# Two softmax attentions, one head at a time or a pair of heads at a time

## The chip, the cores and the metric

The kernel runs on one core of a Trainium2 chip. TensorE (PE in the profile, with its weight loads as PEld) multiplies into PSUM; VectorE (DVE), ScalarE (ACT) and GpSimd (POOL) do the element-wise work; SyncE (SP) issues the transfers. The metric is the device time of the whole program in microseconds (us), the median of several runs.

## The reference, cut to what matters

One program computes two transformer blocks on 512 tokens of width 1024. The first has a neighbourhood attention (8 heads of 64) and a gated convolution; the second an RWKV time mix and, in its second layer, a sliding-window attention with sinks (16 query heads of 64 over 4 key heads). Both attentions are plain softmax attentions:

```python
# neighbourhood attention, first block
s = jnp.einsum('brjqhd,brjkhd->bhrjqk', qb, kb).astype(jnp.float32) * (dh ** -0.5)
s = jnp.where(jnp.asarray(mask), s + bias[None], NEG_INF)
p = jax.nn.softmax(s, axis=-1).astype(v.dtype)
o = jnp.einsum('bhrjqk,brjkhd->brjqhd', p, vb)
...
# sliding window of 128 with a sink per head, second block
s = jnp.einsum('bnqkgd,bnskd->bnkgqs', q, kb).astype(jnp.float32) * (ATT_HEAD ** -0.5)
s = jnp.where(valid[None, :, None, None], s, MASK_VALUE)
p = jax.nn.softmax(jnp.concatenate([s, sink], axis=-1), axis=-1)[..., :-1]
o = jnp.einsum('bnkgqs,bnskd->bnqkgd', p.astype(vb.dtype), vb)
```

## The kernel before

Every projection is a chain of matmuls over 128-wide blocks of the contraction. A weight block is split into a high and a low part (tiles `wh`, `wl`, made by ACT and DVE or POOL from the loaded `wr`), and each block product is three matmuls (`mm3`), written to a PSUM tile named `m`. Other products and transposes go to PSUM tiles named `t`. There are four banks of each kind, taken in turn by `PS()`.

The attentions are written as generators, one for each unit of work, and run between the projection matmuls. A small planner (`_Emit`) keeps a model of each engine's time; a unit is resumed when the tiles that it waits for should be ready. `attention(units, depth)` keeps `depth` units going. All that a unit issues is recorded at line 290 (the branch for urgent work), while other work is at line 288; matmuls are at line 377 and transposes at 391. A scheduler then lays out each engine's own list in order; engines meet by semaphores.

A unit is one head `e` (0 or 1) of a pair of heads and one block `j` of 128 queries. The two heads of a pair share tiles of 128 partitions, head 0 in partitions 0 to 63 and head 1 in 64 to 127, so that their products use different parts of the 128 x 128 array. A unit has these steps:

- scores on PE. In the neighbourhood attention (`na_unit`) that is one fp32 matmul with 64 rows (`t<-a,a`, 64x256), in rows 64e of the array. In the window attention (`sw_unit`) it is two matmuls of 128 rows over a stacked high and low part (`t<-kd,a`)
- add the mask or bias, with the row's minimum of the negated scores, on DVE (CUSTOM_DVE_ANT_0 in the profile, ISA in the order; it frees the scores' bank); exp with its sum on ACT; reciprocal and scaling on DVE
- transposes on PE (`t<-cst,h`), and their copy from PSUM on ACT
- values on PE: for each of two key blocks `kc` one fp32 matmul with 64 columns (`t<-h,a` or `t<-h,vsh`, 64 columns by 128), in columns 64e. The first query block of the window attention has one key block.

There are 32 units of the first kind, run while the convolution's projections are made, and 64 of the second. Half of these (`att0`) run beside the last four blocks of the query projection and the first products of the output projection, the other half (`att1`) beside the output projection. The values of a pair of heads collect in one bank (`po`), from which `split` makes the high and low parts.

Of the kernel before, what the change touches and what calls it, by code (L numbers as in the profile page):

```python
# [295 lines left out]
def tile_net(ctx: ExitStack, tc: tile.TileContext, a: dict, out: bass.AP, dbg=None, stop=None):  # L296
# [359 lines left out]
    def na_unit(hp, j, e):  # L656
        hd = 2 * hp + e
        pr = slice(64 * e, 64 * e + 64)

        def unit():  # L660
            if hd not in bias_t:
                bias_t[hd] = bias_p.tile([P, 768], F32, tag="bias", name=nm("bias"))
                dma(out=bias_t[hd], in_=a["bias1"][:, hd * 768 : (hd + 1) * 768])
            qs, ks = qT[hp][pr, j * 128 : (j + 1) * 128], kT[hp][pr, G0[j] * 64 : G0[j] * 64 + 256]
            yield (qs, ks)
            ps = PS()
            mm(ps[:, 0:256], qs, ks)
            s_, st_ = H(), S()

            vt.tensor_tensor_reduce(out=s_, in0=ps[:, 0:256], in1=bias_t[hd][:, VAR[j] * 256 : VAR[j] * 256 + 256],  # L670
                                    scale=-1.0, scalar=-NEG, op0=ADD, op1=ALU.min, accum_out=st_[:, 1:2])
            act.activation(out=s_, in_=s_, func=AF.Exp, scale=-1.0, bias=st_[:, 1:2], accum_out=st_[:, 2:3])
            vt.reciprocal(out=st_[:, 3:4], in_=st_[:, 2:3])
            vt.tensor_scalar(out=s_, in0=s_, scalar1=st_[:, 3:4], scalar2=None, op0=MUL)
            yield (s_,)
            pt = PS()
            for kc in range(2):
                transpose(pt[:, kc * 128 : (kc + 1) * 128], s_[:, kc * 128 : (kc + 1) * 128])
            pT = H()
            copy(pT, pt[:, 0:256])  # L680
            yield (pT,)
            if hp not in po_t:
                po_t[hp] = [PS(), 0]
            po = po_t[hp][0]
            for kc in range(2):
                mm(po[pr, j * 128 : (j + 1) * 128], vg[G0[j] + 2 * kc][:, hd * 64 : hd * 64 + 64],
                   pT[:, kc * 128 : (kc + 1) * 128], kc == 0, kc == 1)
            po_t[hp][1] += 1
            if po_t[hp][1] == 8:
                ya[hp] = split(po)  # L690
# [4 lines left out]
    with tc.tile_pool(name="bpool", bufs=3) as bias_p:  # L695
        att = em.spawn(attention([na_unit(hp, j, e) for hp in range(4) for j in range(4) for e in range(2)], 5))
# [1246 lines left out]
    def sw_unit(n, j, e):  # L1943
        g, hd = n // 2, 2 * n + e
        pr = slice(64 * e, 64 * e + 64)
        k0, nk, m0 = (0, 128, 128) if j == 0 else ((j - 1) * 128, 256, 0)

        def unit():
            while not q_ready[n]:
                yield 0.25  # L1950
            qs, ks = qts[n][e][:, j * 128 : (j + 1) * 128], [t_[:, k0 : k0 + nk] for t_ in kd[g]]
            yield (qs, *ks)
            ps = PS()
            for i in range(2):
                mm(ps[:, 0:nk], qs, ks[i], i == 0, i == 1)

            s_, st_ = HX(), S()
            gp.tensor_copy(s_[:, nk : nk + 1], nsink[:, hd : hd + 1])
            vt.tensor_tensor_reduce(out=s_[:, 0:nk], in0=ps[:, 0:nk], in1=swam[:, m0 : m0 + nk], scale=-1.0,
                                    scalar=nsink[:, hd : hd + 1], op0=ADD, op1=ALU.min, accum_out=st_[:, 1:2])  # L1960
            act.activation(out=s_[:, 0 : nk + 1], in_=s_[:, 0 : nk + 1], func=AF.Exp, scale=-1.0, bias=st_[:, 1:2],
                           accum_out=st_[:, 2:3])
            vt.reciprocal(out=st_[:, 4:5], in_=st_[:, 2:3])
            vt.tensor_scalar(out=s_[:, 0:nk], in0=s_[:, 0:nk], scalar1=st_[:, 4:5], scalar2=None, op0=MUL)
# [183 lines left out]
```

## Time and profile before

| | |
|---|---|
| median of 3 runs | 3024.93 us (3023.22 to 3025.7) |
| profiled execution | 3018.23 us |
| its span in the trace | 3016.5 us |
| PE busy | 2855.6 us, 95% |
| DVE, ACT, POOL busy | 54%, 42%, 23% |
| neighbourhood attention, first score to last value | 84.9 to 144.6 us |
| window attention, first score to last value | 2491.5 to 2606.5 us |

A page of the profile shows each engine's busy time as a share of the span. A matmul's duration includes its way through the array, so that neighbours overlap; what a matmul costs is read as the distance from its start to the next one's start. One fp32 product stands as two records in the trace: 64 fp32 score products or value products of a stretch would be 128 records.

### The profile page before, as it was taken

How to read it: one execution, taken by the hardware profiler on the slowest of the kernel's cores; microseconds unless marked ns; L12 is line 12 of the kernel's file. 1: busy time of each engine (PE TensorE's matmuls, PEld its weight loads, DVE VectorE, ACT ScalarE, POOL GpSimd, SP SyncE). 2: the span in 40 equal slices, each digit the busy share in tenths (PEclk: the TensorE clock that was granted, in tenths of full speed). 3: DMA queues.
4: the chain of work that ended last, by engine and by line, in shares of the span. 5: the costliest groups of instructions: out<-in, count | busy, mean ns of one | idle time of the engine just before them, and what ended most of it. 6: DMA issues, size and time to landing. Idle time of an engine off the chain costs nothing. (4 is left out here: it accounts for less than half of the span.)

```text
span 3016.5 us, 45856 instructions
## 1 busy us (share of the span) xinstructions
PE 2855.6 (95%) x17744; PEld 2458.6 (82%) x17744; DVE 1628.5 (54%) x2920; ACT 1255.9 (42%) x2205; POOL 690.3 (23%) x809
## 2 busy tenths in 40 slices
PE   9999999999999988788889999998999989899998
PEld 7688888889788876557669999998888887788887
DVE  6544543335334496685866765366234566752336
ACT  4533333323433345454455644344233347643333
POOL 0011211111211143464254210011111134321111
PEclk9999999999999999899779999999999999999999
DMA  5233323332334355655465566343334432323334
GB/s 179 79 98 98 119 91 98 98 98 73 103 98 125 109 177 188 186 172 165 136 177 159 187 178 179 112 152 107 98 98 120 128 102 79 99 81 101 106 109 156
DMA packets 179409, 378.32 MB, mean 125 GB/s; under 512 B 57204, under 2 KB 81908, under 8 KB 179192
## 3 DMA queue, kind: packets, MB, share of 16 engines
q1 hardware_dynamic: 179192, 375.40, 41.6%
q8 instruction: 140, 2.29, 0.3%
q14 instruction: 77, 0.63, 0.1%
HBM read 342.04 MB, written 29.36 MB: 123 GB/s over the span
## 5 line engine op out<-in xcount | busy, mean ns | idle before, releaser
L377 PE MATMUL m<-a,wh 128*128 128x256 f32 (+1 forms) x8512 | 2070.5, 335 | 6.7 <-DVE a L288 4.7
L377 PEld LDWEIGHTS m<-a,wh 128*128 128x128 f32 x8512 | 1462.7, 192 | 171.3 <-issue 10.2
L377 PE MATMUL m<-a,wl 128*128 128x256 f32 (+1 forms) x4256 | 1417.5, 333 | 2.5 <-DVE wl L288 2.3
L288 ACT ACTIVATE wh<-wr 128x1024 fp32r<-128x1024 f32 (+2 forms) x585 | 606.5, 1038 | 1214.0 <-PE m L377 842.0
L288 DVE TENSOR_TENSOR wl<-wr,wh 128x1024 fp32r<-128x1024 f32 (+2 forms) x547 | 673.9, 1233 | 467.7 <-ACT wh L288 464.1
L377 PEld LDWEIGHTS m<-a,wl 128*128 128x128 f32 x4256 | 816.0, 192 | 79.3 <-DVE wl L288 3.9
L288 POOL TENSOR_TENSOR a<-a,a 128x256 f32<-128x256 f32 (+5 forms) x319 | 362.4, 1143 | 1562.0 <-ACT a L288 1335.1
L288 DVE TENSOR_TENSOR a<-m,a 128x512 f32<-128x512 f32 (+1 forms) x324 | 208.7, 645 | 638.8 <-PE m L377 620.9
L288 ACT ACTIVATE a<-a 128x512 f32<-128x512 f32 (+6 forms) x531 | 253.4, 494 | 120.0 <-DVE a L288 100.7
L377 PE MATMUL m<-wh,a 128*128 128x512 f32 x800 | 266.8, 408 | 21.8 <-POOL a L288 9.2
L377 PEld LDWEIGHTS m<-wh,a 128*128 128x128 f32 x800 | 154.6, 194 | 61.9 <-POOL a L288 11.7
L288 DVE TENSOR_TENSOR a<-a,a 128x256 f32<-128x256 f32 (+3 forms) x305 | 159.6, 550 | 24.0 <-ACT a L288 17.2
L377 PE MATMUL m<-wl,a 128*128 128x512 f32 x400 | 161.1, 403 | 0.2 <-DVE wl L288 0.2
L288 DVE SCALAR_TENSOR_TENSOR a<-a,vec,a 128x256 f32<-128x256 f32 (+4 forms) x246 | 145.3, 631 | 8.7 <-ACT a L288 8.4
L288 POOL TENSOR_TENSOR a<-h,a 128x256 fp32r<-128x256 f32 x80 | 70.3, 882 | 292.4 <-ACT a L288 276.3
L288 POOL TENSOR_TENSOR wl<-wr,wh 128x1024 fp32r<-128x1024 f32 x38 | 92.6, 2438 | 134.4 <-ACT wh L288 116.7
L377 PE MATMUL t<-a,a 64*128 64x128 f32 (+3 forms) x400 | 83.7, 380 | 28.0 <-DVE a L288 15.8
L288 ACT ACTIVATE a<-t 128x512 f32<-128x512 f32 (+3 forms) x122 | 58.4, 490 | 86.3 <-PE t L377 68.9
L377 PEld LDWEIGHTS t<-a,a 64*128 64x128 f32 (+2 forms) x400 | 53.2, 222 | 49.2 <-ACT a L288 19.0
L377 PEld LDWEIGHTS m<-wl,a 128*128 128x128 f32 x400 | 77.7, 194 | 16.4 <-issue 0.7
L288 ACT ACTIVATE a<-a,vec 128x256 fp32r<-128x256 f32 (+2 forms) x108 | 60.3, 565 | 41.4 <-DVE a L288 39.2
L377 PE MATMUL t<-cst,a 32*32 32x32 f32 (+2 forms) x432 | 34.7, 237 | 41.4 <-POOL a L288 25.3
(109 smaller groups left out, 1616.2 us busy)
## 6 DMA issues: line engine op xcount, KB each, us to landing
wr<-in_ffn_w_in_dram SPq DMA_DIRECT2D x204, 512.0 KB, 3.7
wr<-in_ffn_w_out_dram SPq DMA_DIRECT2D x80, 448.0 KB, 3.4
wr<-in_ffn_w_out_dram SPq DMA_DIRECT2D x48, 512.0 KB, 3.6
wr<-in_w_out_t_dram SPq DMA_DIRECT2D x34, 512.0 KB, 3.7
wr<-in_w_mlp_in_dram SPq DMA_DIRECT2D x32, 512.0 KB, 3.7
wr<-in_w_mlp_out_dram SPq DMA_DIRECT2D x32, 512.0 KB, 3.7
wr<-in_w_gate_dram SPq DMA_DIRECT2D x16, 512.0 KB, 3.6
wr<-in_w_k_dram SPq DMA_DIRECT2D x16, 512.0 KB, 4.4
```

The lines of the kernel that those rows point to most:

```text
L288: return fn(*args, **kw)
L377: nc.tensor.matmul(out_, lhsT=lhsT, rhs=rhs, start=start, stop=stop)
```

## The change

A unit is now a pair of heads. It has the scores of both heads, their softmax, four transposes into one bank (two in the first query block of the window attention), one copy of up to 512 columns in place of two of up to 256, and the value products in the order key block, then head, so that neighbours alternate between the two halves of the array. The copy goes to a tile of the large pool (`A()`) instead of the pool `h`. In the neighbourhood attention the two heads' scores take a bank each; in the window attention they take the two halves of one bank. `depth` goes from 5 heads to 3 pairs, and the pool of the biases from 3 to 4 tiles.

```diff
@@ -653,47 +653,56 @@
     ya = [None] * 4
     bias_t, po_t = {}, {}
 
-    def na_unit(hp, j, e):
-        hd = 2 * hp + e
-        pr = slice(64 * e, 64 * e + 64)
+    def na_unit(hp, j):
+
+        HE = [(e, slice(64 * e, 64 * e + 64)) for e in range(2)]
 
         def unit():
-            if hd not in bias_t:
-                bias_t[hd] = bias_p.tile([P, 768], F32, tag="bias", name=nm("bias"))
-                dma(out=bias_t[hd], in_=a["bias1"][:, hd * 768 : (hd + 1) * 768])
-            qs, ks = qT[hp][pr, j * 128 : (j + 1) * 128], kT[hp][pr, G0[j] * 64 : G0[j] * 64 + 256]
+            for hd in (2 * hp, 2 * hp + 1):
+                if hd not in bias_t:
+                    bias_t[hd] = bias_p.tile([P, 768], F32, tag="bias", name=nm("bias"))
+                    dma(out=bias_t[hd], in_=a["bias1"][:, hd * 768 : (hd + 1) * 768])
+            qs, ks = qT[hp][:, j * 128 : (j + 1) * 128], kT[hp][:, G0[j] * 64 : G0[j] * 64 + 256]
             yield (qs, ks)
-            ps = PS()
-            mm(ps[:, 0:256], qs, ks)
-            s_, st_ = H(), S()
-
-            vt.tensor_tensor_reduce(out=s_, in0=ps[:, 0:256], in1=bias_t[hd][:, VAR[j] * 256 : VAR[j] * 256 + 256],
-                                    scale=-1.0, scalar=-NEG, op0=ADD, op1=ALU.min, accum_out=st_[:, 1:2])
-            act.activation(out=s_, in_=s_, func=AF.Exp, scale=-1.0, bias=st_[:, 1:2], accum_out=st_[:, 2:3])
-            vt.reciprocal(out=st_[:, 3:4], in_=st_[:, 2:3])
-            vt.tensor_scalar(out=s_, in0=s_, scalar1=st_[:, 3:4], scalar2=None, op0=MUL)
-            yield (s_,)
+            pss = [PS(), PS()]
+            for e, pr in HE:
+                mm(pss[e][:, 0:256], qs[pr, :], ks[pr, :])
+            s2, st_ = [H(), H()], S()
+            for e, ps in enumerate(pss):
+
+                vt.tensor_tensor_reduce(out=s2[e], in0=ps[:, 0:256], in1=bias_t[2 * hp + e][:, VAR[j] * 256 : VAR[j] * 256 + 256],
+                                        scale=-1.0, scalar=-NEG, op0=ADD, op1=ALU.min, accum_out=st_[:, e : e + 1])
+                act.activation(out=s2[e], in_=s2[e], func=AF.Exp, scale=-1.0, bias=st_[:, e : e + 1],
+                               accum_out=st_[:, 2 + e : 3 + e])
+            for e in range(2):
+                vt.reciprocal(out=st_[:, 4 + e : 5 + e], in_=st_[:, 2 + e : 3 + e])
+                vt.tensor_scalar(out=s2[e], in0=s2[e], scalar1=st_[:, 4 + e : 5 + e], scalar2=None, op0=MUL)
+            yield tuple(s2)
             pt = PS()
-            for kc in range(2):
-                transpose(pt[:, kc * 128 : (kc + 1) * 128], s_[:, kc * 128 : (kc + 1) * 128])
-            pT = H()
-            copy(pT, pt[:, 0:256])
+            for e in range(2):
+                for kc in range(2):
+                    transpose(pt[:, (2 * e + kc) * 128 : (2 * e + kc + 1) * 128], s2[e][:, kc * 128 : (kc + 1) * 128])
+            pT = A()
+            copy(pT, pt)
             yield (pT,)
             if hp not in po_t:
                 po_t[hp] = [PS(), 0]
             po = po_t[hp][0]
             for kc in range(2):
-                mm(po[pr, j * 128 : (j + 1) * 128], vg[G0[j] + 2 * kc][:, hd * 64 : hd * 64 + 64],
-                   pT[:, kc * 128 : (kc + 1) * 128], kc == 0, kc == 1)
+                for e, pr in HE:
+                    hd = 2 * hp + e
+                    mm(po[pr, j * 128 : (j + 1) * 128], vg[G0[j] + 2 * kc][:, hd * 64 : hd * 64 + 64],
+                       pT[:, (2 * e + kc) * 128 : (2 * e + kc + 1) * 128], kc == 0, kc == 1)
+            free(pT)
             po_t[hp][1] += 1
-            if po_t[hp][1] == 8:
+            if po_t[hp][1] == 4:
                 ya[hp] = split(po)
 
         return unit
 
     yb, mg = [], []
-    with tc.tile_pool(name="bpool", bufs=3) as bias_p:
-        att = em.spawn(attention([na_unit(hp, j, e) for hp in range(4) for j in range(4) for e in range(2)], 5))
+    with tc.tile_pool(name="bpool", bufs=4) as bias_p:
+        att = em.spawn(attention([na_unit(hp, j) for hp in range(4) for j in range(4)], 3))
 
         r2 = A()
         tt(vt, r2, rb, rb, MUL)
@@ -1940,44 +1949,52 @@
 
     so_t = {}
 
-    def sw_unit(n, j, e):
-        g, hd = n // 2, 2 * n + e
-        pr = slice(64 * e, 64 * e + 64)
+    def sw_unit(n, j):
+
+        g = n // 2
         k0, nk, m0 = (0, 128, 128) if j == 0 else ((j - 1) * 128, 256, 0)
 
         def unit():
             while not q_ready[n]:
                 yield 0.25
-            qs, ks = qts[n][e][:, j * 128 : (j + 1) * 128], [t_[:, k0 : k0 + nk] for t_ in kd[g]]
-            yield (qs, *ks)
+            qs, ks = [qts[n][e][:, j * 128 : (j + 1) * 128] for e in range(2)], [t_[:, k0 : k0 + nk] for t_ in kd[g]]
+            yield (*qs, *ks)
             ps = PS()
-            for i in range(2):
-                mm(ps[:, 0:nk], qs, ks[i], i == 0, i == 1)
-
-            s_, st_ = HX(), S()
-            gp.tensor_copy(s_[:, nk : nk + 1], nsink[:, hd : hd + 1])
-            vt.tensor_tensor_reduce(out=s_[:, 0:nk], in0=ps[:, 0:nk], in1=swam[:, m0 : m0 + nk], scale=-1.0,
-                                    scalar=nsink[:, hd : hd + 1], op0=ADD, op1=ALU.min, accum_out=st_[:, 1:2])
-            act.activation(out=s_[:, 0 : nk + 1], in_=s_[:, 0 : nk + 1], func=AF.Exp, scale=-1.0, bias=st_[:, 1:2],
-                           accum_out=st_[:, 2:3])
-            vt.reciprocal(out=st_[:, 4:5], in_=st_[:, 2:3])
-            vt.tensor_scalar(out=s_[:, 0:nk], in0=s_[:, 0:nk], scalar1=st_[:, 4:5], scalar2=None, op0=MUL)
-            yield (s_,)
-            pt = PS()
-            for kc in range(nk // 128):
-                transpose(pt[:, kc * 128 : (kc + 1) * 128], s_[:, kc * 128 : (kc + 1) * 128])
-            pT = H()
-            copy(pT[:, 0:nk], pt[:, 0:nk])
+            s2, st_ = [HX(), HX()], S()
+            for e in range(2):
+                for i in range(2):
+                    mm(ps[:, e * 256 : e * 256 + nk], qs[e], ks[i], i == 0, i == 1)
+            for e in range(2):
+
+                sink, mn, sm = nsink[:, 2 * n + e : 2 * n + e + 1], st_[:, e : e + 1], st_[:, 2 + e : 3 + e]
+                gp.tensor_copy(s2[e][:, nk : nk + 1], sink)
+                vt.tensor_tensor_reduce(out=s2[e][:, 0:nk], in0=ps[:, e * 256 : e * 256 + nk], in1=swam[:, m0 : m0 + nk], scale=-1.0,
+                                        scalar=sink, op0=ADD, op1=ALU.min, accum_out=mn)
+                act.activation(out=s2[e][:, 0 : nk + 1], in_=s2[e][:, 0 : nk + 1], func=AF.Exp, scale=-1.0, bias=mn, accum_out=sm)
+            for e in range(2):
+                vt.reciprocal(out=st_[:, 4 + e : 5 + e], in_=st_[:, 2 + e : 3 + e])
+                vt.tensor_scalar(out=s2[e][:, 0:nk], in0=s2[e][:, 0:nk], scalar1=st_[:, 4 + e : 5 + e], scalar2=None, op0=MUL)
+            yield tuple(s2)
+            pt, nc_ = PS(), nk // 128
+            for e in range(2):
+                for kc in range(nc_):
+                    i = e * nc_ + kc
+                    transpose(pt[:, i * 128 : (i + 1) * 128], s2[e][:, kc * 128 : (kc + 1) * 128])
+            pT = A()
+            copy(pT[:, 0 : 2 * nk], pt[:, 0 : 2 * nk])
             yield (pT,)
             hf, jj = j // 2, j % 2
             if (n, hf) not in so_t:
                 so_t[n, hf] = [PS(), 0]
             po = so_t[n, hf][0]
-            for kc in range(nk // 128):
-                mm(po[pr, jj * 128 : (jj + 1) * 128], vsh[k0 // 128 + kc][:, g * 64 : g * 64 + 64],
-                   pT[:, kc * 128 : (kc + 1) * 128], kc == 0, kc == nk // 128 - 1)
+            for kc in range(nc_):
+                for e in range(2):
+                    i = e * nc_ + kc
+                    mm(po[HP[e], jj * 128 : (jj + 1) * 128], vsh[k0 // 128 + kc][:, g * 64 : g * 64 + 64],
+                       pT[:, i * 128 : (i + 1) * 128], kc == 0, kc == nc_ - 1)
+            free(pT)
             so_t[n, hf][1] += 1
-            if so_t[n, hf][1] == 4:
+            if so_t[n, hf][1] == 2:
                 split_into(zs[n], po[:, 0:256], HALF[hf])
 
         return unit
@@ -1985,13 +2002,13 @@
     pss = gemm_head(a["w_q"], range(4), en_a.xs, en_a.full)
     ws = [q_out(n, pss[n]) for n in range(4)]
     em.until(lambda: all(w_["done"] for w_ in ws))
-    att0 = em.spawn(attention([sw_unit(n, j, e) for n in range(DC) for j in range(2) for e in range(2)], 5))
+    att0 = em.spawn(attention([sw_unit(n, j) for n in range(DC) for j in range(2)], 3))
     for n in range(4, DC):
         ps = PS()
         gemm(ps, a["w_q"], n, (0, 8), en_a.xs, eng=gp)
         q_out(n, ps)
     em.until(lambda: att0["done"])
-    att1 = em.spawn(attention([sw_unit(n, j, e) for n in range(DC) for j in range(2, 4) for e in range(2)], 5))
+    att1 = em.spawn(attention([sw_unit(n, j) for n in range(DC) for j in range(2, 4)], 3))
     o = [A() for _ in range(DC)]
     so = Stat()
     en = Entry("norm_g", 48 + 32)```

No other instruction is added or taken away: the numbers of matmuls and of DVE, POOL and SP instructions are as before, and ACT has 48 fewer. Outside the two attentions every engine's list stands in the order of before. Three places in the lists follow. The numbers behind tile names only tell tiles apart.

PE in the neighbourhood attention of before, some 3 us after the first transposes: `t_834` is the values' bank of the first pair of heads, `h` tiles are the transposed weights of one head and block, `t_839`, `t_849` and `t_861` are scores of one head.

```order
L391 MATMUL t_829<-cst,h_788 128x128 x2
L377 MATMUL t_834<-h_806,a_720 64x128
L377 MATMUL t_834<-h_806,a_722 64x128
L377 MATMUL t_834<-h_814,a_720 64x128
L377 MATMUL t_834<-h_814,a_722 64x128
L377 MATMUL t_839<-a_634,a_453 128x256
L377 MATMUL t_834<-h_822,a_728 64x128
L377 MATMUL t_834<-h_822,a_731 64x128
L377 MATMUL t_849<-a_634,a_453 128x256
L377 MATMUL t_834<-h_827,a_728 64x128
L377 MATMUL t_834<-h_827,a_731 64x128
```

The same place now, with `a_816`, `a_829` and `a_844` the transposed weights of a pair.

```order
L377 MATMUL t_834<-a_816,a_720 64x128 x2
L377 MATMUL t_834<-a_816,a_722 64x128 x2
L391 MATMUL t_839<-cst,h_788 128x128 x2
L391 MATMUL t_839<-cst,h_789 128x128 x2
L377 MATMUL t_846<-a_634,a_453 128x256
L377 MATMUL t_847<-a_634,a_453 128x256
L377 MATMUL t_834<-a_829,a_728 64x128 x2
L377 MATMUL t_834<-a_829,a_731 64x128 x2
L377 MATMUL t_869<-a_641,a_460 128x256
L377 MATMUL t_870<-a_641,a_460 128x256
L377 MATMUL t_834<-a_844,a_731 64x128 x2
```

Before, the first two units' values stood together and then single heads' scores and values took turns; now scores and values always stand as pairs, and pairs take turns. Counted over the whole stage, PE had 19 bursts of scores and 26 of values, in 21 runs between matmuls of the full array; it now has 15 and 14, in 13 runs.

DVE at the same place now: `t_846` and `t_847` are the scores of one pair, `t_869` and `t_870` of the next; a TENSOR_SCALAR scales a head's weights.

```order
L290 ISA h_850,s_852<-t_846,bias_750 128x256
L290 ISA s_852 128x1
L290 ISA h_851,s_852<-t_847,bias_752 128x256
L290 ISA s_852 128x1
L290 RECIPROCAL s_852<-s_852 128x1
L290 TENSOR_SCALAR h_850<-h_850,s_852 128x256
L290 ISA h_873,s_875<-t_869,bias_865 128x256
L290 ISA s_875 128x1
L290 RECIPROCAL s_852<-s_852 128x1
L290 ISA h_874,s_875<-t_870,bias_867 128x256
```

The first mask instruction of the second pair stands behind the reciprocal and the scaling of the first pair's first head. Before, the list had one head's mask, then the next head's, and only then the first reciprocal.

PE in the window attention, before, where its first values stand (`vsh` are values, `kd` keys; `t_23402` is the values' bank of the first pair of heads):

```order
L391 MATMUL t_23398<-cst,h_23331 128x128
L377 MATMUL t_23402<-h_23366,vsh_19824 64x128
L391 MATMUL t_23404<-cst,h_23341 128x128 x2
L377 MATMUL t_23409<-kd_19796,a_23215 128x128
L377 MATMUL t_23409<-kd_19797,a_23215 128x128
L391 MATMUL t_23419<-cst,h_23354 128x128
L377 MATMUL t_23402<-h_23384,vsh_19824 64x128
L377 MATMUL t_23402<-h_23384,vsh_19826 64x128
L377 MATMUL t_23402<-h_23400,vsh_19824 64x128
L377 MATMUL t_23426<-kd_19796,a_23214 128x256
```

And now (`m_23436` is a block of the query projection):

```order
L377 MATMUL t_23355<-a_23332,vsh_19760 64x128 x2
L377 MATMUL m_23436<-a_22309,wh_23438 128x512
L377 MATMUL t_23355<-a_23339,vsh_19760 64x128 x2
L377 MATMUL t_23355<-a_23339,vsh_19762 64x128 x2
L377 MATMUL t_23364<-a_23347,vsh_19760 64x128 x2
L377 MATMUL t_23367<-kd_19732,a_23150 128x256
L377 MATMUL t_23367<-kd_19733,a_23150 128x256
L377 MATMUL t_23367<-kd_19732,a_23151 128x256
```

Values of single heads, apart from each other, have become pairs. Over the whole stage the values' bursts go from 53 to 31. Of the matmuls that stand between the attention's own, the last of the query projection (`m`, 128x512) stood behind the scores of the seventh pair of heads before; now it stands ahead of the scores of the fourth, and from there to the end of `att0` only products of the output projection stand between, each of which needs the finished values of earlier pairs.

## Rows read from the trace of the kernel before

**Rows 1.** The page, part 1: PE's busy time, share and instructions

```profile
PE 2855.6 (95%) x17744; PEld 2458.6 (82%) x17744; DVE 1628.5 (54%) x2920; ACT 1255.9 (42%) x2205; POOL 690.3 (23%) x809
```

**Rows 2.** Stretches: length; busy PE, PEld, DVE, ACT, POOL; granted clock, DMA share, GB/s

```profile
84.90:145.10 60.20, 59.59 (x340) 39.47 (x340) 36.15 (x143) 36.39 (x108) 3.81 (x6) 1.00 0.28 78
2491.50:2549.30 57.80, 53.89 (x316) 39.15 (x316) 34.68 (x140) 41.37 (x124) 29.71 (x49) 0.94 0.34 90
2549.30:2606.50 57.20, 55.37 (x412) 45.52 (x411) 37.08 (x145) 43.29 (x127) 16.62 (x32) 1.00 0.21 66
2494.00:2501.00 7.00, 5.28 (x16) 3.80 (x16) 3.50 (x17) 4.00 (x13) 4.85 (x3) 0.51 0.79 211
```

**Rows 3.** Waits of PE, 84.9 to 145.1: waiter, releaser, us, times, longest

```profile
PE t L391 <- DVE s L290: 0.4, 1, 0.4
```

**Rows 4.** PE in order of time, neighbourhood attention: start, us, records merged (x)

```profile
84.93 1.92 PE L377 MATMUL t<-a,a 64*128 64x256 f32 x10
...
91.57 0.67 PE L377 MATMUL t<-h,a 128*64 128x128 f32 x8
92.16 0.70 PE L377 MATMUL t<-a,a 64*128 64x256 f32 x2
92.79 0.65 PE L377 MATMUL t<-h,a 128*64 128x128 f32 x4
93.37 0.70 PE L377 MATMUL t<-a,a 64*128 64x256 f32 x2
...
101.12 0.70 PE L377 MATMUL t<-a,a 64*128 64x256 f32 x4
...
112.38 1.13 PE L377 MATMUL t<-a,a 64*128 64x256 f32 x6
...
137.87 0.70 PE L377 MATMUL t<-a,a 64*128 64x256 f32 x2
...
143.65 0.40 PE L377 MATMUL m<-a,wl 128*128 128x512 f32 x1
143.97 0.65 PE L377 MATMUL t<-h,a 128*64 128x128 f32 x4
144.55 0.73 PE L377 MATMUL m<-a,wh 128*128 128x512 f32 x2
145.12 0.40 PE L377 MATMUL m<-a,wl 128*128 128x512 f32 x1
145.36 0.39 PE L377 MATMUL m<-a,wh 128*128 128x512 f32 x1
```

**Rows 5.** PE in order of time, window attention

```profile
2494.27 1.06 PE L377 MATMUL m<-a,wh 128*128 128x512 f32 x2
...
2497.48 0.66 PE L377 MATMUL t<-kd,a 128*128 128x128 f32 x2 [1.72 <-DMA a<-a]
...
2501.95 0.43 PE L377 MATMUL t<-h,vsh 128*64 128x128 f32 x2
2502.31 0.44 PE L391 MATMUL t<-cst,h 128*128 128x128 f32 x2
...
2605.61 0.92 PE L377 MATMUL t<-h,vsh 128*64 128x128 f32 x8
2606.47 0.39 PE L377 MATMUL m<-a,wh 128*128 128x256 f32 x1
```

**Rows 6.** Groups of DVE, 84.9 to 145.1: count, busy us, mean ns, idle before

```profile
L290 DVE CUSTOM_DVE_ANT_0 h<-t,bias 128x256 f32<-128x256 f32 x32 | 13.0, 417 | 18.0 <-PE t L377 17.5 <-DMA bias<-in_bias_dram 0.3
L290 DVE TENSOR_SCALAR h<-h,s 128x256 f32<-128x256 f32 x32 | 11.1, 353 | 0.6
```

**Rows 7.** Groups of ACT: exp in the first attention, copies there, wider copies elsewhere

```profile
L290 ACT ACTIVATE h<-h,s 128x256 f32<-128x256 f32 x32 | 16.1, 504 | 12.8 <-DVE s L290 12.5
L290 ACT ACTIVATE h<-t 128x256 f32<-128x256 f32 x32 | 11.6, 379 | 7.5 <-PE t L391 7.1
L288 ACT ACTIVATE a<-t 128x512 f32<-128x512 f32 x64 | 36.7, 593 | 27.6 <-PE t L391 16.6 <-PE t L377 10.8
```

## The prediction

> **What bounds the kernel now.** I read the page first, for the engine that is nearest to full, then the stretches of the two attentions, then PE's waits there, and last PE's own instructions in order of time. PE is busy for 95% of the span [rows 1]. In the neighbourhood attention it is busy for 59.59 of 60.20 us while DVE and ACT have 36 us each; in the two halves of the window attention it has 53.89 of 57.80 and 55.37 of 57.20, with ACT next at 41.37 and 43.29 [rows 2]. PE's one wait in the first attention that the view of waits shows is 0.4 us [rows 3]. So both stretches are PE's, with some room in the second one, mostly in its start: there PE waits 1.72 us for a transfer, and in the 7 us around it the granted clock is 0.51, the lower of the two levels [rows 2, 5]. What the change is worth is therefore what it saves in PE's list, less what PE must newly wait for.
>
> Busy time overlaps, so I price by distances between starts [rows 4]. A lone head's values (two fp32 products, x4) cost 93.37 - 92.79 = 0.58 us. Two heads that stand behind each other (x8) cost 92.16 - 91.57 = 0.59: the second head is free, although its products stand behind both of the first head's. A lone head's scores cost 92.79 - 92.16 = 0.63; two heads (x4) are busy 0.70 like one (x2), so 0.63 as well; three heads (x6) take 1.13, so a second step costs 0.43. So before, heads already shared the array wherever the list put them side by side, in either order of their products. What the change brings is that all of them stand side by side. A run of such products also costs at its borders, because the matmuls of the full array around it are further apart: 143.97 - 143.65 = 0.32 against 145.36 - 145.12 = 0.24 ahead of it, and 0.57 against 0.48 for two behind it, together 0.17 a run [rows 4].
>
> **The change, part by part.**
>
> Scores of the first attention. Before: 19 bursts, from 84.93 to 137.87, 15.1 us from start to start. Twelve are lone heads (12 x 0.63), three are pairs (1.9), three have three heads, one has five, and 0.9 us of the sum is waiting. Now there are 12 pairs, one pair torn in two, and one burst of three pairs: 12 x 0.63 + 2 x 0.63 + (0.63 + 2 x 0.43) = 10.3. Saved: **4.8**.
>
> Values of the first attention. Before: 26 bursts, from 91.57 to 143.97, of which 6 are pairs: 6 x 0.59 + 20 x 0.58 = 15.1. Now 16 pairs at 0.59 at most: 9.4. Saved: **5.7**.
>
> Borders there: 21 runs become 13, 8 x 0.17 = **1.4**.
>
> Values of the second attention. Before: 53 bursts, from 2501.95 to 2605.61, 29.2 us from start to start. One key block of a head costs 2502.31 - 2501.95 = 0.36 [rows 5], two 0.58, so 0.11 for each further record. The new list has 31 bursts, counted by how deep the deeper head is: 9 of one key block, 17 of two, 3 of three (0.80), 2 of four (1.02): 3.2 + 9.9 + 2.4 + 2.0 = 17.5. Saved: **11.7**.
>
> Borders there: 53 runs become 31, 22 x 0.17 = **3.7**. The scores there use all 128 rows, so pairing saves them nothing.
>
> Together 27.3 us of PE's list.
>
> Edits that I cost at nothing: 80 of ACT's copies of 256 columns at 0.38 us become 40 of 512 at 0.59, and 16 narrower ones become 8 [rows 7]; ACT gains 30.4 - 23.6 = 6.8 us, which matter only if ACT is the bound. The copies' tiles move to the larger pool, which leaves the pool `h` emptier; that hides behind PE's own work, and if a tile there were late a value product would wait at most for another copy, 0.59. A fourth bias tile needs no new transfer.
>
> What PE newly waits for. A pair's scores in the first attention take two of the four banks, and one bank holds values. At the start the fifth head waited for the first mask to free a bank: 1.92 - (0.70 + 2 x 0.43) = 0.36. Now the sixth waits for the second mask too, 0.42 more [rows 4, 6]: 0.8 in all. Later, three pairs' scores alternate with values. The third pair's second bank comes free when the second pair's first mask is done, and DVE's list has put that behind the first pair's scaling: mask 0.42, exp 0.50, scaling 0.35, mask 0.42 [rows 6, 7], with hand-overs, the reading of sums and a reciprocal put at 0.6, is 2.3. PE covers 0.59 + 0.63 + 0.59 = 1.8 of it. That is 0.5 for every three pairs, 2.5 in all, so **3.3** here. The bounds are nothing (DVE overtakes) and twice that.
>
> In the second attention the pair's transposes wait for the second head's exp, 0.50 later than for one head. From the fourth n to the end of `att0`, ten pairs, no products of the query projection stand between to cover it. I take 0.4 for each, **4.0**; the bounds are nothing and the second head's exp and scaling uncovered, 0.85 each, 8.5. The start keeps its waits: it needs the same transfers, and now both heads' at once, with more projection matmuls ahead of them.
>
> Sum: 27.3 - 3.3 - 4.0 = **20.0 us**; the bounds give 27.3 and 27.3 - 6.6 - 8.5 = 12.2. The profiled execution has 3018.23 us (span 3016.5 and 1.7 around it), 6.7 below the median of the runs, 3024.93. So 2998 for an execution like the profiled one, and **3005** for the median.
>
> **Rules of the Trainium skill.** "TensorEngine Tiling (Array Packing)", section PSUM Bottleneck, warns that tiling speeds up TensorE but not the emptying of PSUM, and this speaks against the change. By it the sum would be that of the first rival below, 12.5 us instead of 20.0. In the trace ACT has some 14 us of room in each half of the second attention [rows 2], so it is not the forecast.
>
> **The rivals.**
>
> The softmax chain becomes the bound of the second attention. For it: ACT at 41.37 and 43.29 of 57 us [rows 2], in-order engines, and a unit that has two heads' exp in series. Against it: there was room, and ACT's copies get fewer. The first attention then still gives 11.9 - 3.3 = 8.6, and the second about a quarter of its 15.4, so 12.5 us: 3012.
>
> Alternation itself pays. Were starts on PE strictly in the list's order, two heads behind each other would have cost three steps of two records, 0.59 + 0.22 = 0.81, and the new order within a pair would gain. The row shows 0.59 [rows 4]. If the new order gained 0.2 us on each of the 40 pairs with two key blocks all the same, that is 8 more: 2997. "TensorE: Matmul & The Clock Gate", section The mechanism, says that matmuls start and end strictly in order; the trace does not bear it out for the two halves of the array.
>
> The saving comes back as waits. The banks and the chain take what PE gives, because units are resumed by a plan and not by need: 3024. For it: only four banks. Against it: that takes 27.3 / 48 = 0.57 us of waiting for every one of the 48 pairs, and PE's whole list of waits in the first attention was 0.4 us [rows 3].
>
> Slower: PE starves in `att0` and loses its clock. Place: from the fourth n on, where only products of the output projection, which need the pairs' own results, stand between. For it: around 2494 a gap of 1.72 us goes with a granted clock of 0.51 over 7 us, and two matmuls that take 0.73 elsewhere take 1.06 [rows 2, 4, 5]. Price: ten sixteenths of PE's 53.9 us there, less its saving, are some 29 us of work, which the lower clock doubles. 29 - 20 = 9 us longer: 3034. It decides once the lower clock holds for more than 20 us of that work. Against it: before, PE's gaps after 2502 were too short and too rare for the clock to fall.
>
> **How the numbers follow.** Forecast 0.58 (2998 to 3012), softmax chain 0.19, alternation 0.05, savings lost 0.10, slower 0.08. 0.2% is 6 us, about what a measurement of this kernel tells from no change. Faster: 0.58 + 0.05 + nearly all of the chain's case, 0.81; same 0.11; slower 0.08. The range leaves out the last two cases and takes in the bounds: 2995 to 3016.
>
> **What would show it.** In the trace of the changed kernel, values should stand as x8 that cost 0.59 and scores as x4 that cost 0.63, with hardly a lone x4 or x2. The first score of the second attention should come some 8.6 us earlier than 2491.5, and from there to the end some 11 us less should pass. PE's waits for DVE in the first attention should be near 3 us, at the third pair of scores. The prediction is wrong if x8 in the new order costs more than 0.59, if PE's idle time in the second attention grows by over 9 us, or if the granted clock there falls below 0.9.

## The result, and the profile after

The changed kernel took 2993.69 us in the median of its first 4 runs (2992.11 to 2994.38), against 3025.31 us for the kernel before, measured with it: a ratio of 0.9895, interval 0.9876 to 0.9913. In a later comparison, on another chip, it took 3000.77 us (6 runs, 2990.9 to 3005.73) against 3029.68, 0.9908 [0.9887, 0.9928]. So it is faster, by 31.6 us the first time and by 28.9 the second. The forecast was 3005, or 20.0 us less, with a range from 2995 to 3016: the sign was right, the size too small; the first median lies just below the range, the second inside it.

The page of the changed kernel, part 1, answers to [rows 1]:

```profile
PE 2832.4 (95%) x17744; PEld 2448.3 (82%) x17744; DVE 1623.5 (54%) x2920; ACT 1250.4 (42%) x2157; POOL 688.6 (23%) x809
```

PE's busy time is 23.2 us less at the same number of instructions, and its share is still 95%; the span went from 3016.5 to 2990.3 us, 26.2 less.

The windows of the changed kernel, columns as in [rows 2]: first the neighbourhood attention over the stretch of [rows 2]; then from its first score to the first transfer of the next weights, called stage 1 from here on; then stage 2, from the projection matmuls just ahead of the window attention to those just behind the output projection; last the ten us from the window attention's first score. The first score itself is no place to cut stage 2: from it to the end the kernel before has 2647 matmul records and the changed kernel 2641, because six projection matmuls have moved ahead of it. So stage 2 starts at the 2660th record from the end and stops at the 1600th, and holds the same 1061 in either kernel.

```profile
84.70:145.00 60.30, 60.16 (x387) 43.05 (x387) 39.60 (x149) 37.31 (x95) 4.20 (x6) 1.00 0.28 84
...
84.80:156.10 71.30, 71.16 (x436) 52.24 (x436) 46.03 (x156) 39.97 (x98) 6.97 (x8) 1.00 0.28 85
...
2477.19:2629.35 152.16, 138.50 (x1061) 120.72 (x1060) 113.83 (x376) 111.04 (x281) 73.06 (x97) 0.97 0.31 93
...
2482.70:2492.70 10.00, 7.97 (x34) 5.96 (x34) 6.74 (x23) 8.01 (x19) 9.18 (x10) 0.83 0.74 207
```

The same stretches in the kernel before:

```profile
84.90:166.70 81.80, 81.19 (x436) 57.31 (x436) 47.19 (x156) 42.04 (x114) 7.51 (x8) 1.00 0.28 80
...
2487.31:2655.49 168.18, 154.13 (x1061) 127.96 (x1060) 115.47 (x376) 114.93 (x313) 70.15 (x100) 0.96 0.29 85
...
2491.50:2501.50 10.00, 7.53 (x26) 5.50 (x27) 4.62 (x21) 6.42 (x16) 7.66 (x6) 0.66 0.73 186
```

Stage 1 is 10.5 us shorter, stage 2 16.0, together 26.5. In both, PE's busy time accounts for it: 10.0 less in stage 1 and 15.6 less in stage 2, where its idle time is nearly the same (168.18 - 154.13 = 14.05 us, then 152.16 - 138.50 = 13.66), and so is the granted clock, 0.96 and 0.97. The first score of the window attention comes 8.9 us earlier, with the six more matmuls ahead of it, and 507.6 us instead of 525.0 pass from there to the end.

PE in order of time, neighbourhood attention of the changed kernel; it answers to [rows 4]:

```profile
84.81 2.26 PE L377 MATMUL t<-a,a 64*128 64x256 f32 x12
87.00 0.73 PE L377 MATMUL m<-a,wh 128*128 128x512 f32 x2
...
92.91 0.66 PE L377 MATMUL t<-a,a 128*64 128x128 f32 x8
93.50 0.66 PE L391 MATMUL t<-cst,h 128*128 128x128 f32 x4
94.08 3.47 PE L377 MATMUL t<-a,a 64*128 64x256 f32 x28
97.49 0.73 PE L377 MATMUL m<-a,wh 128*128 128x512 f32 x2
...
103.22 3.27 PE L377 MATMUL t<-a,a 64*128 64x256 f32 x28
106.42 0.73 PE L377 MATMUL m<-a,wh 128*128 128x512 f32 x2
...
121.98 3.47 PE L377 MATMUL t<-a,a 64*128 64x256 f32 x28
125.38 0.73 PE L377 MATMUL m<-a,wh 128*128 128x512 f32 x2
...
133.15 2.16 PE L377 MATMUL t<-a,a 128*64 128x128 f32 x28
135.25 0.73 PE L377 MATMUL m<-a,wh 128*128 128x512 f32 x2
```

A pair's values, x8, cost 93.50 - 92.91 = 0.59, as two heads behind each other did before. A group of x28 is three pairs' scores alternating with two pairs' values; without a wait it takes 3 x 0.63 + 2 x 0.59 = 3.07. The distances to the next start are 3.41 and 3.20, so PE waited 0.34 and 0.13 there; a third such run, from 121.98 to 125.38, waited 0.33. The x28 at 133.15 is three pairs' values and one pair's scores, 2.10, and waited for nothing. The first burst, 87.00 - 84.81 = 2.19, holds 0.70 of waiting beside its 1.49 of work. That is 1.5 us of new waits in the whole stage.

The view of PE's waits in stage 2, first of the kernel before, then of the changed one: waiter, releaser, us in total, times, longest.

```profile
PE t L377 <- POOL a L288: 6.2, 1, 6.2
PE t L377 <- ACT a L288: 1.8, 2, 1.1
PE t L377 <- DMA a<-a: 1.7, 1, 1.7
PE t L391 <- DVE s L290: 1.3, 2, 1.2
PE t L377 <- DVE h L288: 1.0, 2, 0.8
PE t L391 <- DVE h L290: 0.7, 1, 0.7
PE t L377 <- DVE a L290: 0.6, 1, 0.6
PE t L391 <- ACT h L290: 0.3, 1, 0.3
```

```profile
PE t L377 <- POOL a L288: 5.6, 1, 5.6
PE t L391 <- DVE s L290: 3.7, 3, 1.7
PE t L377 <- ACT a L288: 1.0, 1, 1.0
PE t L391 <- DVE h L290: 1.0, 2, 0.7
PE t L377 <- ACT a L290: 0.9, 1, 0.9
PE t L377 <- DMA a<-a: 0.7, 1, 0.7
PE t L391 <- ACT a L288: 0.4, 1, 0.4
PE t L391 <- ACT h L290: 0.2, 1, 0.2
```

The transposes (L391) wait 5.3 us, nearly all of it for the softmax chain, where they waited 2.3; and values wait 0.9 once for their pair's copy (ACT a L290), as none did before. That is 3.9 of new waits, where the prediction priced those of the transposes at 4.0. But the other waits, for ACT and the transfer at the start, for DVE, and for POOL at the end, fell from 11.3 to 7.3 and gave it back. PE's rows in order of time show where the waits at the start and the two longest of the transposes stand, first the kernel before, then the changed one:

```profile
2491.54 0.69 PE L377 MATMUL t<-kd,a 128*128 128x128 f32 x4 [1.12 <-ACT a L288]
...
2493.63 0.84 PE L377 MATMUL t<-kd,a 128*128 128x128 f32 x4 [0.71 <-ACT a L288]
```

```profile
2482.68 0.41 PE L377 MATMUL t<-kd,a 128*128 128x128 f32 x2 [1.02 <-ACT a L288]
2483.80 1.10 PE L377 MATMUL t<-kd,a 128*128 128x128 f32 x6 [0.71 <-DMA a<-a]
...
2541.47 0.41 PE L391 MATMUL t<-cst,h 128*128 128x128 f32 x2 [1.65 <-DVE s L290]
...
2561.21 0.41 PE L391 MATMUL t<-cst,h 128*128 128x128 f32 x2 [1.40 <-DVE s L290]
```

### The profile page after: what moved, and what is told of

It is laid out like the page before. It is cut to its first block, busy times and chain, and to the rows that moved or that the text cites. A ratio compares the mean times of both kernels' runs of the same rounds, so it can differ in the third digit from the quotient of the medians.

```text
span 2990.3 us, 45732 instructions
## 1 busy us (share of the span) xinstructions
PE 2832.4 (95%) x17744; PEld 2448.3 (82%) x17744; DVE 1623.5 (54%) x2920; ACT 1250.4 (42%) x2157; POOL 688.6 (23%) x809
## 5 line engine op out<-in xcount | busy, mean ns | idle before, releaser
L377 PE MATMUL m<-a,wh 128*128 128x256 f32 (+1 forms) x8512 | 2068.2, 335 | 7.2 <-DVE a L288 4.8
L377 PEld LDWEIGHTS m<-a,wh 128*128 128x128 f32 x8512 | 1463.7, 192 | 171.8 <-issue 8.4
L377 PE MATMUL m<-a,wl 128*128 128x256 f32 (+1 forms) x4256 | 1415.3, 333 | 3.6 <-DVE wl L288 3.3
L288 ACT ACTIVATE wh<-wr 128x1024 fp32r<-128x1024 f32 (+2 forms) x585 | 606.5, 1038 | 1190.6 <-PE m L377 814.6
L288 DVE TENSOR_TENSOR wl<-wr,wh 128x1024 fp32r<-128x1024 f32 (+2 forms) x547 | 672.6, 1231 | 467.7 <-ACT wh L288 464.6
L377 PEld LDWEIGHTS m<-a,wl 128*128 128x128 f32 x4256 | 816.2, 192 | 79.6 <-DVE wl L288 5.0
L288 POOL TENSOR_TENSOR a<-a,a 128x256 f32<-128x256 f32 (+5 forms) x319 | 361.9, 1141 | 1645.6 <-ACT a L288 1321.6
L288 DVE TENSOR_TENSOR a<-m,a 128x512 f32<-128x512 f32 (+1 forms) x324 | 208.3, 644 | 636.6 <-PE m L377 619.0
L288 ACT ACTIVATE a<-a 128x512 f32<-128x512 f32 (+6 forms) x531 | 253.3, 495 | 120.7 <-DVE a L288 101.1
L377 PE MATMUL m<-wh,a 128*128 128x512 f32 x800 | 269.6, 412 | 22.4 <-POOL a L288 9.5
L377 PEld LDWEIGHTS m<-wh,a 128*128 128x128 f32 x800 | 156.5, 197 | 63.2 <-POOL a L288 11.8
L288 DVE TENSOR_TENSOR a<-a,a 128x256 f32<-128x256 f32 (+3 forms) x305 | 165.5, 569 | 25.1 <-ACT a L288 18.2
L377 PE MATMUL m<-wl,a 128*128 128x512 f32 x400 | 162.6, 406 | 0.2 <-DVE wl L288 0.2
L288 DVE SCALAR_TENSOR_TENSOR a<-a,vec,a 128x256 fp32r<-128x256 f32 (+4 forms) x246 | 147.7, 640 | 8.6 <-ACT a L288 8.3
L288 POOL TENSOR_TENSOR a<-h,a 128x256 fp32r<-128x256 f32 x80 | 68.1, 855 | 293.2 <-ACT a L288 277.8
L288 POOL TENSOR_TENSOR wl<-wr,wh 128x1024 fp32r<-128x1024 f32 x38 | 92.8, 2444 | 129.1 <-ACT wh L288 97.8
L377 PE MATMUL t<-a,a 64*128 64x128 f32 (+4 forms) x528 | 91.8, 361 | 31.8 <-DVE a L288 21.8
L377 PEld LDWEIGHTS t<-a,a 64*128 64x128 f32 (+3 forms) x528 | 59.3, 202 | 57.5 <-issue 24.5
L288 ACT ACTIVATE a<-t 128x512 f32<-128x512 f32 (+3 forms) x122 | 58.5, 490 | 95.3 <-PE t L377 73.3
L377 PEld LDWEIGHTS m<-wl,a 128*128 128x128 f32 x400 | 78.8, 197 | 16.9 <-issue 0.7
L288 ACT ACTIVATE a<-a,vec 128x256 fp32r<-128x256 f32 (+2 forms) x108 | 60.3, 566 | 41.3 <-DVE a L288 39.2
L290 ACT ACTIVATE a<-t 128x256 f32<-128x256 f32 (+3 forms) x100 | 45.5, 473 | 65.4 <-PE t L377 47.3
```

The costliest lines, as they stand in the source:

```text
L288: return fn(*args, **kw)
L290: return fn(*args, **kw)
L377: nc.tensor.matmul(out_, lhsT=lhsT, rhs=rhs, start=start, stop=stop)
```

## The experiments

The two stages in all traces, cut at the same places of the list as above, with the medians (e1 to e3 and the changed kernel stand against a kernel before of 3025.31 us, e4 likewise, e5 to e7 against 3025.23, e8 and e9 against 3029.68):

| kernel | stage 1, us | stage 2, us | median, us | ratio to before |
|---|---|---|---|---|
| before | 81.8 | 168.2 | 3025.31 | |
| before again (e1) | 81.8 | 167.9 | 3026.78 | 1.0007 [0.9997, 1.0016] |
| first attention only (e2) | 71.2 | 168.4 | 3013.16 | 0.9959 [0.9944, 0.9974] |
| second only (e3) | 81.8 | 152.4 | 3009.57 | 0.9942 [0.9927, 0.9957] |
| changed | 71.3 | 152.2 | 2993.69 | 0.9895 [0.9876, 0.9913] |
| changed again (e8) | 71.3 | 152.1 | 3000.77 | 0.9908 [0.9887, 0.9928] |
| same half (e4) | 81.7 | 164.8 | 3020.75 | 0.9981 [0.9969, 0.9993] |
| head, then key block (e5) | 72.2 | 151.9 | 2998.02 | 0.9919 [0.9898, 0.9940] |
| the same again (e9) | 72.2 | 152.1 | 2998.05 | 0.9903 [0.9879, 0.9926] |
| four pairs going (e6) | 72.7 | 153.9 | 2999.48 | 0.9918 [0.9904, 0.9932] |
| before, six heads going (e7) | 81.4 | 167.6 | 3022.14 | 0.9991 [0.9979, 1.0002] |

**The kernel before, unaltered.** No edit; it shows what a difference must exceed.

> The kernel of before, unchanged, run and profiled once more. Theory: the profiled execution of before (3018.23 us) lay 6.7 us under its timed runs (3024.93) because the granted clock fell for less of it; another execution should come out near 3025, and its trace should show the attentions as before (values of the first attention 15.2 us in 26 bursts, of the second 29.2 us in 53) and the difference in stretches at the lower clock. Rival: the 6.7 us are in the attentions themselves (transfers or waits that come and go there), and then the attentions' stretches differ by that much between two executions of the same kernel.

Its runs go from 3022.22 to 3033.78 us, and its profiled execution has a span of 3029.4 us, 12.9 more than that of before, with the very same lists. The windows of one stretch of the RWKV time mix show where, first in before, then in this run:

```profile
1050.00:1500.00 450.00, 364.34 (x2808) 292.47 (x2807) 337.69 (x653) 218.99 (x445) 189.64 (x244) 0.89 0.56 171
```

```profile
1050.00:1500.00 450.00, 369.44 (x2766) 295.50 (x2764) 323.58 (x619) 214.63 (x432) 187.32 (x240) 0.86 0.55 169
```

In the same 450 us, in which PE has 81 to 86 us of gaps, the granted clock is 0.89 in one execution and 0.86 in the other, and the second shows 42 matmul records less. The first score of the window attention, ahead of which nothing differs in the program, comes at 2491.5 us in before and, by PE's rows in order of time, 14.2 us later here:

```profile
2505.71 0.70 PE L377 MATMUL t<-kd,a 128*128 128x128 f32 x4 [2.14 <-DMA a<-a]
```

So a time of one execution says little below some 10 us, while the length of a stage that both executions share holds to 0.1 us in stage 1 and 0.3 us in stage 2.

**Each attention alone.** One of the two units as before, the other as changed.

> Only the neighbourhood attention works on pairs, the window attention on single heads. Theory (heads side by side in PE's list): the stage of the first attention gets 10.7 us shorter, as in the changed kernel, and the median is about 3025 - 11 = 3014. Rival (fewer copies and less load on ACT matter): only 16 of 48 copies go here, so a third of 31.6 us, also about 10 us, but then without shorter bursts of PE. Rival (clock): the median moves by 11 us plus or minus up to 6 us of stretches at the lower clock elsewhere.

> Only the window attention works on pairs. Theory: its stretch from the first score to the output projection's end gets some 16 us shorter (11 of values, 3.7 of borders, 1.7 of lower clock), median about 3009, and the sum with the run that changes only the first attention is 27 us, not the 31.6 us that were measured for both; the rest is clock. If the sum is 31.6 us within 2 us, nothing is left for the clock and one of the two stretches is mis-measured by the profile of before.

The first gives 12.2 us by the medians and 10.6 in its stage; the second 15.7 by the medians and 15.8 in its stage. Each leaves the other's stage as it was, to 0.2 us. The two savings of the medians add to 27.9, the two stages' to 26.4: the parts are independent, and no third place shows a gain.

**A pair in one half of the array.** Two query blocks of one head make a pair, with the same depth, banks, number of copies and softmax as in the changed kernel; what differs for PE is the second member's place in the array. (In `att0` a pair is one block with one key block and one with two, so that its copies are 384 columns wide.)

```diff
-    def na_unit(hp, j):
-        HE = [(e, slice(64 * e, 64 * e + 64)) for e in range(2)]
+    def na_unit(hp, jp, e):
+        hd, pr = 2 * hp + e, slice(64 * e, 64 * e + 64)
+        JS = (2 * jp, 2 * jp + 1)
...
-            for e, pr in HE:
-                mm(pss[e][:, 0:256], qs[pr, :], ks[pr, :])
+            for i, j in enumerate(JS):
+                mm(pss[i][:, 0:256], qT[hp][pr, j * 128 : (j + 1) * 128], kT[hp][pr, G0[j] * 64 : G0[j] * 64 + 256])
...
-    def sw_unit(n, j):
+    def sw_unit(n, hf, e):
```

> A unit is two blocks of queries of one head instead of one block of two heads: the same number of units, of copies, of transposes in a bank, the same depth, but both halves of the unit need the same part of the array. Theory (the array is shared by neighbours in different parts): scores and values cost about as much as with single heads (first attention 15 us each, second about 27 us), only borders get fewer (7 and 24 runs at 0.17 us): 5 to 8 us faster than before, 3017 to 3020. Rival (the gain comes from larger units: half the copies, half the bursts, fewer switches of the list): at least 20 us faster than before, 3005 or less.

PE's rows in order of time, the same place as above:

```profile
92.78 1.09 PE L377 MATMUL t<-a,a 128*64 128x128 f32 x8
93.80 0.66 PE L391 MATMUL t<-cst,h 128*128 128x128 f32 x4
94.39 5.01 PE L377 MATMUL t<-a,a 128*64 128x128 f32 x28
99.33 0.73 PE L377 MATMUL m<-a,wh 128*128 128x512 f32 x2
```

The same eight value records cost 93.80 - 92.78 = 1.02 us instead of 0.59, and the run of three pairs 4.94 instead of 3.41. Stage 1 keeps the length of before, which had six pairs of both halves by chance, and stage 2 gives 3.4 us (at a granted clock of 0.94 in its window, against 0.96, so perhaps a few us short of what it could). The median is 4.6 us below the kernel before, a little less than the 5 to 8 that I expected. So fewer and longer bursts, wider copies and 48 fewer ACT instructions are worth little by themselves; the gain needs the second head in the other half.

**The order inside a pair.** Values by head, then key block, so that neighbours no longer alternate; run twice, the second time beside the changed kernel on one chip.

```diff
-            for kc in range(2):
-                for e, pr in HE:
+            for e, pr in HE:
+                for kc in range(2):
...
-            for kc in range(nc_):
-                for e in range(2):
+            for e in range(2):
+                for kc in range(nc_):
```

> The changed kernel with a pair's values in the order head, then key block, so that the two products of a head stand behind each other as before and nothing alternates. Theory (each part of the array takes its own products, whatever the order of neighbours): a burst of a pair still costs 0.59 us, and the time is that of the changed kernel, 2994, within 3 us (the scheduler's list changes a little, with 9 and 12 bursts instead of 15 and 14 in the first attention, for up to 1 us less). Rival (alternation pays): a burst costs 0.59 + 0.22 = 0.81 us, 8 us slower than the changed kernel, 3002.

> The pair's value products in the order head, then key block, against the changed kernel's on the same chip. Theory (the halves of the array have queues of their own, so the order inside a pair is worth nothing): within 3 us of the changed kernel's median, the value bursts of two key blocks cost 0.59 us again. Rival (neighbours must alternate): the 16 pairs of the first attention and 22 of the second with two or more key blocks cost 0.2 us more each, 8 us slower than the changed kernel, and bursts at 0.81 in the trace.

PE's rows in order of time in the second run of it:

```profile
93.09 0.66 PE L377 MATMUL t<-a,a 128*64 128x128 f32 x8
93.68 0.66 PE L391 MATMUL t<-cst,h 128*128 128x128 f32 x4
94.27 3.74 PE L377 MATMUL t<-a,a 128*64 128x128 f32 x28
97.93 0.73 PE L377 MATMUL m<-a,wh 128*128 128x512 f32 x2
```

The burst costs 0.59 again. Stage 1 is 0.9 us longer, stage 2 the same within 0.3, and the medians on one chip are 2998.05 and 3000.77, closer than their spreads. The alternation in the change's name is worth nothing that can be measured; standing side by side is. The planner laid the list out a little differently around the pairs; which of these rows made the 0.9 us in stage 1 was not parted.

**More units at once.** Four pairs going in place of three, and in the kernel before six heads in place of five.

```diff
-    att = em.spawn(attention([na_unit(hp, j) for hp in range(4) for j in range(4)], 3))
+    att = em.spawn(attention([na_unit(hp, j) for hp in range(4) for j in range(4)], 4))
```

> The changed kernel with four pairs in flight instead of three, in both attentions. PE's list has 10 bursts of scores and 14 of values in the first attention (15 and 14 with three) and 27 of values in the second (31). Theory: the bursts and borders save about 1 to 2 us, and with four pairs the late transposes of the second attention (some 9 us of waiting in the changed kernel after its start) find more cover: 2985 to 2992. Rival (four banks are the limit): seven or eight scores behind each other wait for masks, 0.4 us each, and the time is 2994 or more.

> The kernel of before with six single heads in flight instead of five, so that an even number starts together. PE's list has 20 bursts of scores and 23 of values in the first attention (19 and 26 before) and 47 of values in the second (53). Theory: what counts is how many heads stand side by side; three values' bursts fewer at 0.58, six fewer at 0.4 to 0.58, and a few borders give 3 to 5 us: 3020 to 3022. Rival (an even depth is all that the change needs): near the changed kernel, under 3005.

Four pairs are no better, 72.7 and 153.9 us in the stages, and the 2985 to 2992 that I expected did not come. PE's rows show a part of the price in the first:

```profile
84.47 2.61 PE L377 MATMUL t<-a,a 64*128 64x256 f32 x14
87.00 0.73 PE L377 MATMUL m<-a,wh 128*128 128x512 f32 x2
...
87.98 0.70 PE L377 MATMUL t<-a,a 64*128 64x256 f32 x2
88.61 0.74 PE L377 MATMUL m<-a,wh 128*128 128x512 f32 x2
```

The fourth pair's first score joins the burst, 87.00 - 84.47 = 2.53, and its second is torn off: it stands behind projection matmuls in the list and costs 88.61 - 87.98 = 0.63 for one head alone. Three pairs' scores already ask for more than the four banks. In the kernel before, a sixth head changes the stages by 0.6 us or less, where I expected 3 to 5, and the time by nothing that can be told from zero: the depth was not what bound it.

**The changed kernel, unaltered.** No edit.

> The changed kernel unaltered, timed in more runs. Theory (two heads side by side save 10.5 us in the first attention and 17 in the second, and the rest of the 31.6 us of the first comparison is TensorE's granted clock between 1050 and 2000 us, which differs from run to run of one and the same list of instructions): the two stages last 71 and 131 us again, the median over more runs lies near 2997, between 2994 and 3000, the runs spread over some 10 us, and the ratio to the kernel before is 0.9905 to 0.9915. Rival (all of the 31.6 us comes from the change, some of it in later stages): the median is 2994 again and all runs lie within 2 us.

Both stages last as long as in the first run, to 0.1 us. The runs spread from 2990.9 to 3005.73, so the narrow 2992 to 2994 of the first four was chance. The first score of the window attention comes at 2494.66 us here and at 2482.68 in the first run, 12.0 us apart; their spans are 3002.4 and 2990.3, 12.1 apart. Both executions are the same program, and all their difference lies ahead of that attention. A part of it stands ahead of 1050 us too: from 780 to 850 us the granted clock is 1.00 in the first execution and 0.95 in this one, and the first 1050 us hold 5223 matmul records there and 5190 here.

## Why the prediction came out too small

**What PE saves: right.** The prediction had 27.3 us gross. In stage 1 it had 4.8 + 5.7 + 1.4 = 11.9; the measured 10.5 with 1.5 of new waits on top make 12.0. In stage 2 it had 11.7 + 3.7 = 15.4; PE's busy time fell by 15.6. Added up from start to start over that stage's rows, waits included, the values went from 29.2 us (53 bursts) to 18.2 (31), 11.0 instead of 11.7. So 5.0 of the 16.0 us lie beside them, where 3.7 were foreseen for borders: 1.4 in the scores, 0.9 in the transposes and 2.7 in the other matmuls of the full array. I had counted the borders of the values alone, while scores stand in 27 bursts instead of 47 and transposes in 55 instead of 60. And I had put a border too low: the 0.48 for two matmuls without a run ahead of them was twice 0.24, and the rows behind those of [rows 4] show 0.45:

```profile
145.36 0.62 PE L377 MATMUL m<-a,wh 128*128 128x512 f32 x2
145.81 0.40 PE L377 MATMUL m<-a,wl 128*128 128x512 f32 x1
```

With it a run costs 0.08 + 0.12 = 0.20 at its borders, and 22 of them 4.4. That the rest is borders was not measured by itself.

**What PE newly waits for: the step that failed.** The sum took off 7.3 us, and about 1.1 would have been right. Two terms of it:

- In the first attention, 3.3 was put and 1.5 measured. The start was right (0.70 against 0.36 + 0.42 = 0.78). The 0.5 at every third pair's scores happened three times, not five, at 0.34, 0.13 and 0.33. One of the five runs of pairs held two pairs of scores and no third; in another, three pairs' values stood first, and gave the bank time to come free.
- In the second attention, 4.0 was put and nothing measured net: PE's idle time in stage 2 is 0.4 us less than before, within the 0.6 by which two executions of before differ. The new waits did come, 3.9, but not as 0.4 at each of ten pairs of `att0`: there PE waited 0.15 and 0.31 at transposes and 0.90 at values. Two of 0.66 come ahead of those ten, at the first transposes of all, and the two longest, 1.65 and 1.40, stand behind the last of `att0`'s 96 value records, in `att1`, for which the prediction put nothing. What failed is that the sum held all the old waits fixed, and said so of the start. Before, the first scores waited 1.12, 0.71 and 1.72 us [rows 5 has the last]; now 1.02 and 0.71, that is 1.8 less (3.1 and 1.7 in the repeats). Another 2.2 went from waits further on that the prediction does not name: 0.6 at scores for DVE, 1.0 at products that wait for DVE behind the attention, and 0.6 at POOL. The start is also less slow: over its first 10 us the granted clock is 0.66 before and 0.83 now, in the repeats as well. More projection matmuls stand ahead of the later scores, as the section on the change shows, and I had counted them as no cover at all; that it is they which cover was not tested by itself.

So the savings less the waits are 20.0 in the prediction and 26.5 in the stages, 0.8 us below the gross sum: a bound that I gave, and not the value that I took. None of my three signs of being wrong appeared: they watched for a change worth less than forecast, and not for one worth more.

**The base.** The remaining 5 us of the first comparison's 31.6 are not in the stages. The change leaves every list outside them in its order, and e1 and e8 show the same program to differ by 12 us between executions, through the granted clock, most of it in the time mix. The 28.9 and 31.6 of the two comparisons are both above 26.5, by less than this spread, and the intervals of both take it in (26.3 to 37.5 us and 21.8 to 34.2). The same holds for the 6.7 us between the profiled execution of before and its median, which the prediction carried over as fixed: it is one draw of that spread. With 26.5 in place of 20.0 the prediction's own base gives 2998 for the median, inside the range; that the first median fell below 2995 took the base as well.

**The rivals.** The softmax chain did not become the bound: ACT is busy 111.04 of 152.16 us in stage 2, PE 138.50. "TensorEngine Tiling (Array Packing)", section PSUM Bottleneck, in the Trainium skill, which warns that tiling does not speed up the emptying of PSUM, stood behind this rival; here PE waited for a pair's copy once, for 0.9 us. That alternation itself pays is refuted by e5 and e9; that its 2997 lies nearest to the first median is chance. By the same runs a lone pair's cost does not follow from starts strictly in the list's order, as "TensorE: Matmul & The Clock Gate" of the Trainium skill, section The mechanism, has it: 0.59 us in either order, where the prediction worked out 0.81 from that rule. The lost saving and the slower kernel were wrong in the same point as the forecast, only more so: PE's idle time in stage 2 did not grow. The granted clock in it is 0.96 before and 0.97 after.

What stays open: which of the projection matmuls now cover the start's waits, and what part of the 5.0 us beside the values is borders. Whether both heads' scores of the first attention can share a bank, and whether that would end the 1.5 us of waits there, was not tried.

## What to carry to other kernels

When products use half of the array, price them by distances between starts: here a neighbour in the other half was free (0.01 us) and one in the same half was not (0.44), in whatever order they stood within the group. Make them neighbours by building the unit of work out of both halves, and expect the saving in PE's list in full as long as PE is the bound and the other engines have room. Before a new wait is taken off a forecast, look at whether the same reordering moves cover to an old wait: idle time is better forecast as a sum over the stage than wait by wait. And cut a stage that two kernels share at the same instruction of both lists, with the same count of records between: the first score was not such a place here.

## What the runs showed of the hardware

One and the same program has spans of 3016.5 and 3029.4 us, the changed one of 2990.3 and 3002.4, with mean granted clocks of 0.967 and 0.961, 0.967 and 0.962. Most of the stretches in which the two levels, 1.2 and 2.4 GHz, alternate are those of the time mix, where PE has gaps; stage 1, at 1.00, repeats to 0.1 us between two executions of one program and stage 2, at 0.96 and 0.97, to 0.3. Differences of a few us are therefore read from a stage, not from the span.

A second head's values cost 0.01 us in the other columns of the array (0.59 against 0.58) and 0.44 in the same ones (1.02).
